# Attention and indexer scores from unsplit q and k, a pair's heads on the two halves of the rows

## The chip, the cores and the metric

The kernel runs on one core of one Trainium2 chip. The metric is the device time of one execution in microseconds. It was taken three times before the change; the median counts.

## What is computed

Two layers (`DEPTH`) of a hybrid block on 256 tokens of width 1024. Each layer projects the normalised input to 6484 columns and feeds four branches: a Mamba-2 branch, and three attention branches of 8 heads with 64 elements each (fox with forget gates, moba, and dsa with an indexer that keeps 64 keys per query). The branches' outputs are gated, projected and summed, and a SwiGLU FFN follows.

```python
DEPTH = 2; SEQ = 256; HEAD_DIM = 64          # 8 heads in fox, moba and dsa, 4 index heads

def fox_branch(q, k, v, f_logit, f_bias):     # causal softmax with a bias cq - cf
    logits = jnp.einsum('bqhd,bkhd->bhqk', qb, k).astype(jnp.float32) * scale
    logits = logits + cq[..., :, None] - cf[..., None, :]
    logits = jnp.where(kpos[None, :] <= qpos[:, None], logits, -jnp.inf)
    p = jax.nn.softmax(logits, axis=-1).astype(v.dtype)
    return jnp.einsum('bhqk,bkhd->bqhd', p, v)

def moba_branch(q, k, v):                     # one block of 256 keys: causal attention
...
def dsa_branch(q, k, v, qi, ki, wi):
    isc = jax.nn.relu(jnp.einsum('bqhd,bkd->bqhk', qib, ki).astype(jnp.float32) * idx_scale)
    isc = jnp.einsum('bqh,bqhk->bqk', wib.astype(jnp.float32) * w_scale, isc)
    isc = jnp.where(kpos[None, None, :] <= qpos[None, :, None], isc, -jnp.inf)
    _, sel = lax.top_k(isc, n_keep)           # n_keep = 64
    ...
    logits = jnp.einsum('bqhd,bqkhd->bqhk', qb, k_sel).astype(jnp.float32) * scale

def hybrid_mixer(...):
    u = h @ w_in                              # 1024 x 6484
    ...                                       # the four branches
    proj = jnp.einsum('bsnc,ncd->bsnd', ys, w_branch)
    gates = jax.nn.sigmoid(h @ w_gate + b_gate).reshape(bsz, seq, N_BRANCH, D_MODEL)
    return jnp.sum(gates * proj, axis=2) @ w_out

def reference(...):
    for l in range(DEPTH):
        h = rms_norm(x, norm_mix_pre[l])
        x = x + rms_norm(hybrid_mixer(h, ...), norm_mix_post[l])
        h = rms_norm(x, norm_ffn_pre[l])
        x = x + rms_norm(swiglu(h, w_ffn_in[l], w_ffn_out[l]), norm_ffn_post[l])
    return x
```

## The kernel before, in words

**Gemms in split form.** Every large product is made of float32r products. A weight is loaded as `raw`, copied by ScalarE to `whi` (line 307), and what the copy lost is subtracted on VectorE to `wlo` (`sub_lo`, line 123). The activations are kept in the same way as a high and a low part (`hh`, `hl`). A gemm adds up high x high, low x high and high x low: `emit_b` makes 24 matmuls of 256 columns for 128 output columns.

**Quanta and ticks.** The work is a list of quanta, each some 24 matmuls of one gemm, in a fixed order. In a mixer it is mv, fv, the small columns, iq (2 quanta), mq (4), mk (4), xs (4), bs (2), cs (2), z (4), fq (4), fk (4), dv, dq, dk, then the gates and branch projections; below, xs2 is the third quantum of xs. The main loop (from line 1134) issues for quantum i the `whi` copy of three quanta ahead and the `wlo` subtraction of two quanta ahead, then the matmuls, then one `tick`. A tick advances every post-processing generator (`posts`) and every active attention generator by one step, so a `yield` means "the next quantum". An engine executes its instructions in the order in which they are issued.

**Attention units.** After the last quantum of mk the four head pairs of moba are put into `units`; the state-space pairs, fox and dsa follow. Every third tick (`STEP`) one unit is started. A unit of `attn_gen` treats two heads, b = 0 and 1, in the steps score (TensorE), low (VectorE: scale, mask and row minimum), expo (ScalarE), recip (VectorE), norm (GpSimd), tr (TensorE), ev (ScalarE), head 1 one tick behind head 0; then come the value product and the split of its result. Ahead of that stand `split_k` and `split_q`, which fill three ticks. They give a product of 128 rows in place of one of 64: the stationary operand `qs` has the query's high part in one half of the rows and its low part in the other, the moving operand `kh` has the key's high part in both, and `klz` has the key's low part in one half and zeros in the other. A head's scores are then two matmuls for each of the two query blocks (128 and 256 keys), and in fox one more each that adds the gate's bias from `csS`.

**The indexer.** `index_gen` makes the scores of four index heads in the same form, sums them with weights into `iacc`, and searches the largest 64 in eight rounds for each query block (`max`, `match_replace` on VectorE), one step a tick. Its result is a mask for dsa.

**The convolution.** The post-processing of xs, bs and cs takes three VectorE steps a quantum (`cacc`, line 585) and one product (`xsc` or `bc`, line 571). That of z has one product, mq and mk have the two steps of `rope`, with GpSimd's part behind them.

**Buffers.** Two pools hold PSUM tiles of one bank each: `pg` has 3 for the gemms, `pa` has 5 for everything else: scores, transposes, value products. Each new tile takes the one that came free first, and its first write waits for the last reader of the old one.

Of the kernel before, what the change touches and what calls it, by code (L numbers as in the profile page):

```python
# [9 lines left out]
F32 = mybir.dt.float32  # L10
# [5 lines left out]
P = 128  # L16
S = 256
# [23 lines left out]
def host_constants():  # L41
    import numpy as np
    c = np.zeros((P, NCST), np.float32)
    p = np.arange(P)
    l = np.arange(S)
    c[:, C_ID:C_ID + P] = np.eye(P, dtype=np.float32)
    c[:, C_TRI:C_TRI + P] = p[:, None] <= p[None, :]
    c[:, C_ONE:C_ONE + P] = 1.0
    c[:, C_MASK:C_MASK + P] = np.where(p[None, :] > p[:, None], BIG, 0.0)
    c[:, C_MASK + P:C_MASK + 3 * P] = np.where(l[None, :] > p[:, None] + P, BIG, 0.0)  # L50
    c[:, C_MASKT:C_MASKT + P] = np.where(p[None, :] < p[:, None], -BIG, 0.0)
    inv = np.power(np.float32(10000.0), -np.arange(0, 64, 2, dtype=np.float32) / np.float32(64)).astype(np.float32)
    ang = (np.arange(S, dtype=np.float32)[:, None] * inv[None, :]).astype(np.float32)
    j = (p % 64) // 2
    c[:, C_COS:C_COS + S] = np.cos(ang).astype(np.float32)[:, j].T
    c[:, C_SIN:C_SIN + S] = np.sin(ang).astype(np.float32)[:, j].T * np.where(p % 2 == 0, -1.0, 1.0)[:, None]
    for r in range(16):
        c[r, C_SEL + r] = 1.0
        c[32 + r, C_SEL + r] = 1.0
    return c  # L60
# [31 lines left out]
def kernel(ctx: ExitStack, tc: tile.TileContext, a, out):  # L92
# [68 lines left out]
    nh = cp.tile([P, 1], F32, name="nh")  # L161
    V.memset(nh, -0.5)
    csS = cp.tile([P, S], F32R, name="csS")
    klz = [cp.tile([P, 2, S], F32R, name=f"klz{i}") for i in range(2)]
    turn = [0]
    par = cp.tile([P, DEPTH, 76], F32, name="par")
    av = cp.tile([P, DEPTH, 16], F32, name="av")
    dsk = cp.tile([P, DEPTH, 4], F32, name="dsk")
# [13 lines left out]

    def clear_pads():
        G.memset(csS.bitcast(F32), 0.0)
        for z in klz:
            G.memset(z.bitcast(F32), 0.0)

    def setup_params():
        V.tensor_copy(sel, cst[:, C_SEL:C_SEL + 16])
        pp = aps()  # L190
        for l in range(DEPTH):
            T.transpose(pp[:, l * P:(l + 1) * P], rows[:, l, :], ident)
        pv = pp[:, 0:2 * P].rearrange("p (l c) -> p l c", l=DEPTH)
        V.tensor_scalar(par[:, :, 0:72], pv[:, :, 0:72], 0.5, None, op0=ALU.mult)
        V.tensor_copy(par[:, :, 72:76], pv[:, :, 72:76])
        V.memset(av, -1.0)
        for l in range(DEPTH):
            ea = tp.tile([P, 8], F32, name="ea")
            A.activation(ea, hd[:, l, 2, :], AF.Exp)
            V.tensor_scalar(av[:, l, 0:8], ea, -1.0, None, op0=ALU.mult)  # L200
            V.tensor_copy(dsk[0:64, l, :], hd[0:64, l, 3, 0:8:2])
            V.tensor_copy(dsk[64:128, l, :], hd[64:128, l, 3, 1:8:2])
# [555 lines left out]

    HALVES = (LOWER, UPPER)

    def split_q(q, scale):
        qs = tp.tile([P, 2, S], F32R, name="qs", bufs=2)
        for b, h in enumerate(HALVES):
            A.activation(qs[h, b, :], q[h], AF.Copy, scale=scale)
        yield
        for b, h in enumerate(HALVES):
            V.scalar_tensor_tensor(qs[HALVES[1 - b], b, :], q[h], scale, qs[h, b, :].bitcast(F32),  # L767
                                   op0=ALU.mult, op1=ALU.subtract)
        return qs

    def split_k(k):
        kh = tp.tile([P, 2, S], F32R, name="kh", bufs=2)
        kl = klz[turn[0] % 2]
        turn[0] += 1
        for b, h in enumerate(HALVES):
            A.activation(kh[h, b, :], k[h], AF.Copy)
        yield
        for b, h in enumerate(HALVES):
            V.tensor_copy(kh[HALVES[1 - b], b, :], kh[h, b, :])
            G.tensor_tensor(kl[h, b, :], k[h], kh[h, b, :].bitcast(F32), op=ALU.subtract)  # L780
        return kh, kl

    def s_mms(ps, b, qs, kh, kl, bias=None):
        for sl, q0, n in QT:
            mm(ps[:, sl], qs[:, b, q0:q0 + P], kh[:, 0:n], True, False)
            mm(ps[:, sl], qs[:, b, q0:q0 + P], kl[:, 0:n], False, bias is None)
            if bias is not None:
                mm(ps[:, sl], selrow(bias), csS[:, 0:n], False, True)

    def index_gen(l, L):  # L790
        yield from wait(("w16", l))
        yield
        ikh = tp.tile([P, S], F32R, name="ikh")
        ikl = tp.tile([P, S], F32R, name="ikl")
        A.activation(ikh, L["ik"], AF.Copy)
        qs = [None, None]
        for i in range(2):
            qs[i] = yield from split_q(L["iq"][:, i, :], 1.0)
        sub_lo(ikl, L["ik"], ikh)
        yield  # L800
        acc = tp.tile([P, 384], F32, name="iacc")
        ps, rl = {}, {}
        for s in range(6):
            if s < 4:
                ps[s] = aps()
                s_mms(ps[s], s % 2, qs[s // 2], ikh, ikl)
            if 0 <= s - 1 < 4:
                rl[s - 1] = t15("irl")
                A.activation(rl[s - 1], ps[s - 1][:, :384], AF.Relu)
            h = s - 2  # L810
            if h >= 0:
                for t, (sl, q0, n) in enumerate(QT):
                    V.scalar_tensor_tensor(acc[:, sl], rl[h][:, sl], L["w16"][:, t, h:h + 1],  # L813
                                           mask[:, sl] if h == 0 else acc[:, sl],
                                           op0=ALU.mult, op1=ALU.subtract if h == 0 else ALU.add)
            yield
        for rnd in range(8):
            for t, (sl, q0, n) in enumerate(QT):
                m8 = tp.tile([P, 8], F32, name="m8", bufs=2)
                V.max(m8, acc[:, sl])  # L820
                V.match_replace(out=acc[:, sl], in_to_replace=m8, in_values=acc[:, sl], imm_value=DROP)  # L821
                yield
        L["dm"] = tp.tile([P, 384], F32, name="dm")
        V.tensor_scalar(L["dm"], acc, DROP * 0.5, BIG, op0=ALU.is_gt, op1=ALU.mult)
        V.tensor_tensor(L["dm"], L["dm"], mask, op=ALU.max)
        flags.add(("dm", l))

    def attn_gen(l, L, br, qk, kk, vk, i, fox, dsa):
        if fox:
            yield from wait(("cs", l))  # L830
        if dsa:
            yield from wait(("dm", l))
        kh, kl = yield from split_k(L[kk][:, i, :])
        qs = yield from split_q(L[qk][:, i, :], -0.125)
        yield
        v = L[vk]
        add = L["dm"] if dsa else mask
        ps, sm, mn, ls, rc, pr, pT, sT = ([None, None] for _ in range(8))

        def score(b):  # L840
            ps[b] = aps()
            s_mms(ps[b], b, qs, kh[:, b, :], kl[:, b, :], 8 + 2 * i + b if fox else None)

        def low(b):
            sm[b] = t15("sm")
            mn[b] = tp.tile([P, 2], F32, name="mn", bufs=4)
            for t, (sl, q0, n) in enumerate(QT):
                V.tensor_tensor_reduce(sm[b][:, sl], ps[b][:, sl], add[:, sl], op0=ALU.add, op1=ALU.min,  # L848
                                       scale=1.0, scalar=3e38, accum_out=mn[b][:, t:t + 1])

        def expo(b):
            pr[b] = tp.tile([P, 384], F32, name="pr", bufs=4)
# [332 lines left out]
```

## Time and profile before

| what | value |
|---|---|
| median of 3 executions | 1130.69 us (1130.31 to 1187.93) |
| the profiled execution | 1132.14 us |
| span of its instructions | 1130.4 us |
| mean granted clock of TensorE | 0.989 |
| busy: TensorE, VectorE, ScalarE, GpSimd | 97%, 68%, 56%, 25% |

The span runs from the first to the last instruction of the profiled execution; the rest of its time lies around it. Busy shares are of the span. Matmuls overlap, and their ends are modelled, so the distance from one start to the next says more than a duration. All times in the rows below are microseconds from the start of the span, unless ns stands there.

### The profile page before, as it was taken

Reading aid. Unit: us, or ns where it says so; the run is one execution under the profiler, and the core shown is the slowest. Engines: PE = TensorE matmul, PEld = TensorE weight load, DVE = VectorE, ACT = ScalarE, POOL = GpSimd, SP = SyncE. Lnnn points to the kernel's source line nnn. Section 1 sums busy time; section 2 is a strip of 40 time slices with the busy share of each in tenths; the row PEclk is TensorE's granted clock in tenths of the full one; section 3 lists DMA queues with packets and bytes.
Section 4 is the critical chain, followed back from the end, with each engine's and each line's share of the span. In section 5 each row is a group of like instructions: output and inputs, shape, how many; then the busy total and the mean of one; then the engine's idle time right before and its main releaser. Section 6 shows DMA issues by size and latency. Waiting matters only on the chain.

```text
span 1130.4 us, 20409 instructions
## 1 busy us (share of the span) xinstructions
PE 1099.5 (97%) x8067; PEld 1031.5 (91%) x8067; DVE 767.1 (68%) x1430; ACT 631.2 (56%) x1190; POOL 277.8 (25%) x327
## 2 busy tenths in 40 slices
PE   7998999999999999999999979999999999999997
PEld 5997889999999799998879979899999988999986
DVE  6799969866547755546478999597754677545542
ACT  6646677676445554445355577757755455454531
POOL 1342337533222100000014424474331320000000
PEclk9998999999999999999999989999999999999999
DMA  7743443454557455556654435345446574565650
GB/s 225 227 150 112 150 149 119 155 163 146 162 191 242 138 185 181 186 188 224 224 141 133 150 112 175 125 135 165 125 155 196 183 238 150 179 195 165 220 194 37
DMA packets 153923, 188.96 MB, mean 167 GB/s; under 512 B 12740, under 2 KB 129764, under 8 KB 153828
## 3 DMA queue, kind: packets, MB, share of 16 engines
q1 hardware_dynamic: 153828, 187.67, 50.7%
q8 instruction: 63, 1.03, 0.4%
q14 instruction: 32, 0.26, 0.1%
HBM read 186.61 MB, written 1.05 MB: 166 GB/s over the span
## 4 chain that ended last, share of the span: by engine, by line
PE 81%; DVE 13%; ACT 3%; issue 2%; POOL 1%; DMA 0%; SPq 0%; DVEq 0%; POOLq 0%; ACTq 0%
PE g L120 61%; PE a L120 18%; DVE wlo L123 4%; DVE cacc L585 2%; PE a L870 2%; ACT junk L238 1%; DVE qs L767 1%; ACT whi L307 1%; DVE rsh L503 1%; POOL pnr L208 1%; DVE iacc L813 0%; DVE rt L504 0%; DVE ny L244 0%; DVE iacc L821 0%; DMA raw<-in_w_in_dram 0%
## 5 line engine op out<-in xcount | busy, mean ns | idle before, releaser
L123 DVE TENSOR_TENSOR wlo<-raw,whi 128x1024 fp32r<-128x1024 f32 (+2 forms) x386 | 444.2, 1170 | 106.6 <-ACT whi L307 84.7
L307 ACT ACTIVATE whi<-raw 128x1024 fp32r<-128x1024 f32 (+2 forms) x386 | 368.6, 986 | 63.9 <-DMA raw<-in_w_ffn_out_dram 37.9
L120 PE MATMUL g<-hh,whi 128*128 128x256 f32 x1776 | 254.9, 287 | 0.0
L120 PE MATMUL g<-hl,whi 128*128 128x256 f32 x1776 | 252.2, 285 | 0.0
L120 PE MATMUL g<-hh,wlo 128*128 128x256 f32 x1776 | 249.6, 283 | 0.0
L120 PEld LDWEIGHTS g<-hh,whi 128*128 128x128 f32 x1776 | 231.0, 193 | 1.3 <-issue 0.7
L120 PEld LDWEIGHTS g<-hl,whi 128*128 128x128 f32 x1776 | 232.1, 194 | 0.0
L120 PEld LDWEIGHTS g<-hh,wlo 128*128 128x128 f32 x1776 | 229.7, 192 | 0.0
L864 POOL TENSOR_SCALAR pr<-pr,rc 128x128 f32<-128x128 f32 x96 | 66.5, 705 | 132.7 <-DVE rc L860 119.0
L150 POOL TENSOR_SCALAR gain<-gain 128x1024 f32<-128x1024 f32 x4 | 4.8, 1207 | 335.6 <-DMA gain<-in_norm_ffn_post_dram 315.0
L643 ACT ACTIVATE gt<-g,par 128x256 f32<-128x256 f32 x64 | 30.3, 474 | 98.8 <-PE g L120 98.8
L663 POOL TENSOR_TENSOR mg<-mg,gt 128x256 f32<-128x256 f32 x48 | 53.5, 1123 | 112.6 <-DVE gt L657 112.6
L1017 DVE TENSOR_TENSOR hu<-gt,g 128x256 f32<-128x256 f32 x40 | 16.9, 421 | 87.0 <-PE g L120 87.0
L120 PE MATMUL a<-whi,hidh 128*128 128x512 f32 x176 | 55.6, 390 | 0.0
L120 PE MATMUL a<-wlo,hidh 128*128 128x512 f32 x176 | 55.5, 389 | 0.0
L120 PE MATMUL a<-whi,hidl 128*128 128x512 f32 x176 | 55.4, 389 | 0.0
L1009 ACT ACTIVATE gt<-g 128x256 f32<-128x256 f32 x40 | 15.4, 385 | 68.0 <-PE g L120 68.0
L506 POOL TENSOR_TENSOR rsh<-rsh,cst 128x256 f32<-128x256 f32 (+1 forms) x38 | 29.5, 777 | 89.3 <-DVE rsh L503 88.9
L657 DVE SCALAR_TENSOR_TENSOR gt<-gt,g 128x256 f32<-128x256 f32 x48 | 19.8, 419 | 40.0 <-PE g L120 34.0
L855 ACT ACTIVATE pr<-sm,mn 128x128 f32<-128x128 f32 x96 | 42.4, 446 | 3.4 <-DVE mn L848 3.4
L120 PE MATMUL g<-whi,hh 128*128 128x512 f32 x128 | 41.3, 404 | 1.6 <-ACT hh L278 1.0
L1019 ACT ACTIVATE hidh<-hu 128x256 fp32r<-128x256 f32 x40 | 16.7, 418 | 45.0 <-DVE hu L1017 45.0
(227 smaller groups left out, 1535.1 us busy)
## 6 DMA issues: line engine op xcount, KB each, us to landing
raw<-in_w_ffn_in_dram SPq DMA_DIRECT2D x40, 1024.0 KB, 5.1
raw<-in_w_in_dram SPq DMA_DIRECT2D x38, 1024.0 KB, 5.0
raw<-in_w_gate_dram SPq DMA_DIRECT2D x32, 1024.0 KB, 5.5
raw<-in_w_ffn_out_dram SPq DMA_DIRECT2D x22, 1024.0 KB, 4.9
raw<-in_w_branch_dram SPq DMA_DIRECT2D x16, 1024.0 KB, 5.0
raw<-in_w_in_dram SPq DMA_DIRECT2D x24, 512.0 KB, 6.3
raw<-in_w_out_dram SPq DMA_DIRECT2D x8, 1024.0 KB, 6.3
raw<-in_w_ffn_in_dram SPq DMA_DIRECT2D x8, 512.0 KB, 5.1
```

Of the source, the lines that this page charges most:

```text
L120: T.matmul(o, l, r, start=start, stop=stop)
L123: V.tensor_tensor(lo, src, hi.bitcast(F32), op=ALU.subtract)
L307: A.activation(dst(c.hi[i]), src(c.raw), AF.Copy)
L506: G.tensor_tensor(sh[:n], sh[:n], sin[:n], op=ALU.mult)
L585: V.scalar_tensor_tensor(ac[:, sft:], u[:, :S - sft], wcol(3 - sft), ac[:, sft:], op0=ALU.mult, op1=ALU.add)
L643: A.activation(th, o, AF.Tanh, bias=par[:, l, 40 + br * 8 + d:41 + br * 8 + d], scale=0.5)
L657: V.scalar_tensor_tensor(L["gt", d], L["gt", d], 1.0, os[j], op0=ALU.add, op1=ALU.mult)
L663: G.tensor_tensor(md, md, L["gt", d], op=ALU.add)
L855: A.activation(pr[b][:, sl], sm[b][:, sl], AF.Exp, bias=mn[b][:, t:t + 1], scale=-1.0, accum_out=ls[b][:, t:t + 1])
L864: G.tensor_scalar(pr[b][:, sl], pr[b][:, sl], rc[b][:, t:t + 1], 1.0, op0=ALU.mult, op1=ALU.mult)
L870: T.transpose(pT[b][:, js], pr[b][:, js], ident)
L1017: V.tensor_tensor(u, H["s", j], o, op=ALU.mult)
```

## The change

The splits of q and k for scores go, with `qs`, `kh`, `klz`, `ikh` and `ikl`. A head's scores become one float32 product of 64 rows for each query block, from the rope results (or, in fox, their copies) directly. Head 0 of a pair has its 64 elements in partitions 0 to 63, head 1 in 64 to 127, so the two lie on the two halves of TensorE's rows. Both heads' scores are issued in one step, each into its own PSUM tile. The factor -1/8 that the split applied to q moves into the instruction of `low`; the masks, the fox bias and the index mask are scaled by -8 to fit. Index heads are treated two at a time in the same way (the index key already stood in both halves of the partitions).

```diff
-    c[:, C_MASK:C_MASK + P] = np.where(p[None, :] > p[:, None], BIG, 0.0)
-    c[:, C_MASK + P:C_MASK + 3 * P] = np.where(l[None, :] > p[:, None] + P, BIG, 0.0)
+    c[:, C_MASK:C_MASK + P] = np.where(p[None, :] > p[:, None], -8 * BIG, 0.0)
+    c[:, C_MASK + P:C_MASK + 3 * P] = np.where(l[None, :] > p[:, None] + P, -8 * BIG, 0.0)
...
-    klz = [cp.tile([P, 2, S], F32R, name=f"klz{i}") for i in range(2)]
-    turn = [0]
...
         G.memset(csS.bitcast(F32), 0.0)
-        for z in klz:
-            G.memset(z.bitcast(F32), 0.0)
...
-        V.memset(av, -1.0)
+        V.memset(av, 8.0)
...
-    def split_q(q, scale):
-        qs = tp.tile([P, 2, S], F32R, name="qs", bufs=2)
...
-    def split_k(k):
-        kh = tp.tile([P, 2, S], F32R, name="kh", bufs=2)
...
-    def s_mms(ps, b, qs, kh, kl, bias=None):
...
+    def scores(q, k, bias=None):
+        ps = [aps(), aps()]
+        for t, (sl, q0, n) in enumerate(QT):
+            for b, h in enumerate(HALVES):
+                mm(ps[b][:, sl], q[h, q0:q0 + P], k[h, 0:n], t == 0, t == 1 and bias is None)
+        if bias is not None:
+            for t, (sl, q0, n) in enumerate(QT):
+                for b in range(2):
+                    mm(ps[b][:, sl], selrow(bias + b), csS[:, 0:n], False, t == 1)
+        return ps
 
     def index_gen(l, L):
         yield from wait(("w16", l))
-        yield
-        ikh = tp.tile([P, S], F32R, name="ikh")
-        ikl = tp.tile([P, S], F32R, name="ikl")
-        A.activation(ikh, L["ik"], AF.Copy)
-        qs = [None, None]
-        for i in range(2):
-            qs[i] = yield from split_q(L["iq"][:, i, :], 1.0)
-        sub_lo(ikl, L["ik"], ikh)
         yield
...
         for s in range(6):
-            if s < 4:
-                ps[s] = aps()
-                s_mms(ps[s], s % 2, qs[s // 2], ikh, ikl)
+            if s in (0, 2):
+                ps[s], ps[s + 1] = scores(L["iq"][:, s // 2, :], L["ik"])
...
-                                           op0=ALU.mult, op1=ALU.subtract if h == 0 else ALU.add)
+                                           op0=ALU.mult, op1=ALU.add)
...
-        V.tensor_scalar(L["dm"], acc, DROP * 0.5, BIG, op0=ALU.is_gt, op1=ALU.mult)
-        V.tensor_tensor(L["dm"], L["dm"], mask, op=ALU.max)
+        V.tensor_scalar(L["dm"], acc, DROP * 0.5, -8 * BIG, op0=ALU.is_gt, op1=ALU.mult)
+        V.tensor_tensor(L["dm"], L["dm"], mask, op=ALU.min)
...
-        kh, kl = yield from split_k(L[kk][:, i, :])
-        qs = yield from split_q(L[qk][:, i, :], -0.125)
-        yield
...
         def score(b):
-            ps[b] = aps()
-            s_mms(ps[b], b, qs, kh[:, b, :], kl[:, b, :], 8 + 2 * i + b if fox else None)
+            if b == 0:
+                ps[:] = scores(L[qk][:, i, :], L[kk][:, i, :], 8 + 2 * i if fox else None)
...
-                                       scale=1.0, scalar=3e38, accum_out=mn[b][:, t:t + 1])
+                                       scale=-0.125, scalar=3e38, accum_out=mn[b][:, t:t + 1])
```

## Rows read from the trace of the kernel before

**Rows 1.** The page: busy time of the engines, and the chain that ended last.

```profile
PE 1099.5 (97%) x8067; PEld 1031.5 (91%) x8067; DVE 767.1 (68%) x1430; ACT 631.2 (56%) x1190; POOL 277.8 (25%) x327
PE 81%; DVE 13%; ACT 3%; issue 2%; POOL 1%; DMA 0%; SPq 0%; DVEq 0%; POOLq 0%; ACTq 0%
```

**Rows 2.** Line 120 (matmuls): TensorE idle until what, us and times.

```profile
  DVE qs L767: 18.9, 10
```

**Rows 3.** Timeline, TensorE, layer 0: start, length, what, count [idle before <-releaser].

```profile
103.48 0.44 PE L120 MATMUL a<-kh,qs 128*128 128x128 f32 x1 [5.22 <-DVE qs L767]
...
117.73 0.33 PE L120 MATMUL a<-kh,qs 128*128 128x128 f32 x1 [1.88 <-DVE qs L767]
```

**Rows 4.** Timeline, TensorE, the second such wait of layer 1.

```profile
673.62 0.33 PE L120 MATMUL a<-kh,qs 128*128 128x128 f32 x1 [1.67 <-DVE qs L767]
```

**Rows 5.** Windows: length, busy us of five engines, TensorE's granted clock, DMA.

```profile
98.30:103.50 5.20, 0.02 (x1) 0.06 (x1) 5.00 (x15) 3.35 (x11) 0.00 (x0) 0.76 0.18 59
103.50:107.90 4.40, 4.40 (x21) 4.40 (x22) 4.26 (x11) 2.85 (x7) 0.24 (x1) 0.51 0.40 118
117.80:122.00 4.20, 4.20 (x23) 4.20 (x24) 4.13 (x9) 4.09 (x12) 0.92 (x1) 0.59 0.22 71
```

**Rows 6.** Timeline, TensorE: one head's scores between two gemms.

```profile
91.88 0.22 PE L120 MATMUL a<-kh,qs 128*128 128x128 f32 x1
91.94 0.27 PE L120 MATMUL a<-klz,qs 128*128 128x128 f32 x1
92.05 0.33 PE L120 MATMUL a<-kh,qs 128*128 128x256 f32 x1
...
92.34 1.12 PE L120 MATMUL g<-hh,whi 128*128 128x256 f32 x8
93.29 1.12 PE L120 MATMUL g<-hl,whi 128*128 128x256 f32 x8
```

**Rows 7.** Timeline, TensorE: full-row float32 products, and the gemm behind them.

```profile
123.12 1.47 PE L120 MATMUL a<-bc 128*128 128x256 f32 x8
124.35 1.20 PE L120 MATMUL g<-hh,whi 128*128 128x256 f32 x8
```

**Rows 8.** Timeline, TensorE: a pair's value product, and the gemm behind it.

```profile
182.27 0.88 PE L120 MATMUL a<-sT,xdt 128*64 128x256 f32 x8
183.08 1.21 PE L120 MATMUL g<-hh,whi 128*128 128x256 f32 x8
```

**Rows 9.** Timeline, GpSimd: the two subtractions for pair 0.

```profile
88.96 2.62 POOL L780 TENSOR_TENSOR klz<-mk,kh 64x256 fp32r<-64x256 f32 x2 [8.46 <-ACT kh L776]
```

**Rows 10.** Timeline, VectorE, in the convolution quanta of layer 0.

```profile
80.71 1.21 DVE L123 TENSOR_TENSOR wlo<-raw,whi 128x1024 fp32r<-128x1024 f32 x1
...
83.27 0.74 DVE L813 SCALAR_TENSOR_TENSOR iacc<-irl,w,iacc 128x128 f32<-128x128 f32 x2
84.04 0.61 DVE L779 CAST kh<-kh 64x256 fp32r<-64x256 f32 x2
...
90.01 0.96 DVE L571 SCALAR_TENSOR_TENSOR xsc<-th,cacc 128x256 f32<-128x256 f32 x1
90.90 2.00 DVE L585 SCALAR_TENSOR_TENSOR cacc<-cu,par,cacc 128x255 f32<-128x255 f32 x3
...
94.80 0.42 DVE L571 SCALAR_TENSOR_TENSOR xsc<-th,cacc 128x256 f32<-128x256 f32 x1
95.14 1.51 DVE L585 SCALAR_TENSOR_TENSOR cacc<-cu,par,cacc 128x255 f32<-128x255 f32 x3
...
101.39 0.42 DVE L820 MAX8 m<-iacc 128x8 f32<-128x256 f32 x1
...
102.25 0.28 DVE L848 CUSTOM_DVE_ANT_0 sm<-a,cst 128x128 f32<-128x128 f32 x1
...
102.91 0.87 DVE L767 SCALAR_TENSOR_TENSOR qs<-mq,qs 64x256 fp32r<-64x256 f32 x2
...
118.16 1.23 DVE L123 TENSOR_TENSOR wlo<-raw,whi 128x1024 fp32r<-128x1024 f32 x1
```

More of the change, by code (lines that the diff above doesn't have):

```diff
@@ L759 @@
     HALVES = (LOWER, UPPER)
-    def split_q(q, scale):
-        qs = tp.tile([P, 2, S], F32R, name="qs", bufs=2)
-        for b, h in enumerate(HALVES):
-            A.activation(qs[h, b, :], q[h], AF.Copy, scale=scale)
-        yield
[L766 to L769, printed above, removed]
-    def split_k(k):
-        kh = tp.tile([P, 2, S], F32R, name="kh", bufs=2)
[L773 to L776, printed above, removed]
-        yield
[L778 to L781, printed above, removed]
-    def s_mms(ps, b, qs, kh, kl, bias=None):
[L784 to L788, printed above, removed]
+    def scores(q, k, bias=None):
[8 more added lines that the diff above has]
+        return ps
     def index_gen(l, L):
         yield from wait(("w16", l))
-        yield
-        ikh = tp.tile([P, S], F32R, name="ikh")
-        ikl = tp.tile([P, S], F32R, name="ikl")
-        A.activation(ikh, L["ik"], AF.Copy)
-        qs = [None, None]
-        for i in range(2):
-            qs[i] = yield from split_q(L["iq"][:, i, :], 1.0)
-        sub_lo(ikl, L["ik"], ikh)
         yield
@@ L832, in attn_gen @@
             yield from wait(("dm", l))
-        kh, kl = yield from split_k(L[kk][:, i, :])
-        qs = yield from split_q(L[qk][:, i, :], -0.125)
-        yield
         v = L[vk]
```

## The prediction, on record before the result

> **What bounds the kernel now.** I read the page first: matmuls keep TensorE busy 97% of the span, and they are most of the chain that ended last, with VectorE next at 13% [rows 1]. So a change counts by what it takes from TensorE's stream and by the waits in it. The second view lists what ended TensorE's idle times: 18.9 us, matmuls and weight loads together, ended with `qs`, the split query that line 767 writes on VectorE [rows 2]. TensorE's timeline shows where. In layer 0 the first product of moba pair 1 waits 5.22 us and that of pair 2 1.88 us [rows 3]; layer 1 repeats both, the second with 1.67 us [rows 4]. From start to start each costs some 0.15 us more than its idle time.
>
> The windows show what comes with such a wait. During the first, VectorE is busy 5.00 of 5.20 us: TensorE waits because VectorE is behind with everything. Afterwards the granted clock is 0.51 of full (the 1.2 GHz level), and 21 matmuls take 4.40 us; after the second wait 23 take 4.20 us at 0.59 [rows 5]. At the usual pace, eight gemm products in 0.95 us [rows 6], these are 2.4 and 2.7 us, so the clock costs 2.0 and 1.5 us. Layer 0 thus loses 5.4 + 2.0 + 2.0 + 1.5 = 10.9 us here, layer 1 some 10.7: 21.6 us, the only large sum that the change can reach.
>
> **TensorE's own work.** A head's scores now take four matmuls, from 91.88 to 92.34 us [rows 6], so 0.92 us a pair (fox adds its bias, which stays). The new pair is four float32 products of 64 rows. The trace has no product of 64 rows, but two neighbours with the same columns (two of 256, two of 128); each float32 product shows as two matmuls. The four full-row products of `bc` in `ssd_prep_gen` are eight matmuls and take 1.23 us [rows 7]. The value products of a pair go to two halves of the columns: again eight, in 0.81 us [rows 8]. So the halves overlap, though all products of one half are written first. Leaving costs something: the gemm group behind lasts 1.21 us where its kind lasts 1.12 [rows 6, 8], and I take the same 0.09 us for entering. A visit costs 0.99 us. The load ahead of the first product has 128 columns, where the value product's has 64; full-row matmuls of 128 columns start 0.11 us apart (91.94 to 92.05), so half of that shows more. I take 1.05 us, +0.13 a pair, since halves of the rows are nearest to halves of the columns. The ends: half of 1.23, 0.62 us (overlap, and neither entry nor exit: -0.30), and 1.23 + 0.18 + two loads of 0.11 = 1.63 us (no overlap: +0.71). Between them: loads of the two halves one behind the other, 8 x 0.11 + 0.18 + the last product, 0.2, = 1.26 us (+0.34).
>
> The Trainium skill (TensorE: Matmul & The Clock Gate, "LDWEIGHTS") says that a load's time goes by its columns and not by its rows, about 107 ns for 128; by that eight loads one behind the other are an estimated 0.86 us. The Trainium skill (TensorEngine Tiling, "Key Properties") says that tiles load and multiply in parallel, which speaks for 1.05 us. The trace has overlapping loads of 64 columns and none of 64 rows, so it decides for neither.
>
> **What leaves the other engines.** For an attention pair ScalarE loses four copies, GpSimd two subtractions (2.62 us for two, beside VectorE [rows 9]) and VectorE two casts, together 0.61 us, and two splits, 0.87 us [rows 10]. `low` keeps its cost: -0.125 stands where 1.0 stood in the same instruction. Masks, `av` and the two cleared pads are set-up that no wait of the list in [rows 2] hangs on.
>
> **What moves.** The split's suspensions go, so a pair's scores come three quanta earlier, and the indexer's too. Their inputs are no wait: pair 0's rope results are written three quanta before. But VectorE's `low`, the search's rounds and GpSimd's `norm` move with them, into the convolution quanta where VectorE is late. And both heads take their PSUM tiles at once.
>
> **The sum in the convolution quanta.** Between the wlo subtractions of quanta xs2 (80.71) and z2 (118.16) VectorE spends 37.45 us on eight quanta [rows 10].
> - Removed: three pairs' casts, 3 x 0.61 = 1.8; three splits, 3 x 0.87 = 2.6; the indexer's last product step, 0.74, now done earlier; and the stretching beside GpSimd's subtractions, where a product took 0.96 us instead of 0.42 and three `cacc` steps 2.00 instead of 1.51 [rows 9, 10]: 1.0, and once more 0.5. Together 6.6.
> - Added: two more `low` steps, 2 x 0.66 (102.25 to 102.91); one more search round, 0.86 (101.39 to 102.25); two reciprocals, some 0.1; two more `norm` steps on GpSimd, whose stretching I put at 1.0 (bounds 0 and 2, by the stretching just named). Together 3.3.
>
> That leaves 37.45 - 6.6 + 3.3 = 34.1 us. For the same quanta TensorE needs 8 x 2.87 us for gemms of 24, two pairs at 1.05, three times three transposes at 0.11 and a value product at 0.99: 27.1 us. VectorE starts xs2 up to 1 us behind. So at z2 it is about 34.1 + 0.5 - 27.1 = 7.5 us behind; TensorE comes to the scores of pair 3 after a gemm and three transposes, 3.2 us later.
>
> **The wait that takes its place.** The five PSUM tiles of pool `pa` go round in the order in which they come free. At z2, pair 0's value product and pair 1's two transposes hold three. Pair 3's scores need both of pair 2's score tiles, and the second is read by `low(1)`, issued in quantum z1 as VectorE's last work there. So pair 3 waits until VectorE ends z1, just as `qs` made pair 2 wait: 7.5 - 3.2 = 4.3 us. Behind the waiting product stand the gemm of z3 and all later matmuls, in order. Pairs 1 and 2 find tiles freed two quanta back or more, and their waits go. After z2 no convolution step is left and VectorE catches up. With 1.6 us for the clock, by the two measured, a layer still loses 5.9 us: two layers gain 21.6 - 11.8 = 9.8 us. An error of 0.3 us in each quantum moves a layer by 2.4 us.
>
> The extra 0.13 us counts only where TensorE doesn't wait for VectorE anyway: not for the index pairs and moba pairs 0 to 2, so for 18 of 28 pairs, +2.3 us. Sum: -7.5 us. The profiled execution took 1132.14 us, of which the span is 1130.4; the median is 1130.69, and I set the difference against that: 1123.2, say 1123 us. Two per cent, 22.6 us, is about what a measurement of this kernel can tell from no change.
>
> **Rivals.**
> 1. The waits vanish. If VectorE's backlog at z2 stays within 3.2 us (no stretching, each quantum 0.4 us cheaper), 21.6 us come back, less 28 x 0.13 = 3.6: 1112.7 us; with pairs at 0.62 us, 1100.7. For: VectorE loses 24 x 1.48 + 4 x 0.87 = 39 us over the kernel. Against: the sum above. Chance 0.18.
> 2. The row halves don't overlap. From 0.92 + 9.8/18 = 1.46 us a pair on the change loses; at 1.63 it is 18 x 0.71 - 9.8 = +3.0: 1133.7 us, slower than before. For: the trace has no such product. Against: column halves overlap, and the two heads write different PSUM tiles. Chance 0.17.
> 3. Loads one behind the other: 18 x 0.34 - 9.8 = -3.7: 1127 us. Chance 0.10.
> 4. The change doesn't do what it says: the wait for a PSUM tile takes back all that the wait for `qs` cost. It needs VectorE 12 us behind at z2, not 7.5. Then +2.3 is left: 1133 us. Chance 0.12.
>
> My forecast, 1117 to 1129, has 0.43. The range takes in rival 1 without its far end and rivals 2 to 4: 1109 to 1137. Faster by over 2% (below 1108) needs rival 1 and cheap pairs at once: 0.09. Slower by over 2% needs over 1 us more for each of 28 pairs than I forecast: 0.03. Within 2%: 0.88.
>
> **What would show it.** No wait for `qs`; none of 5 us ahead of pair 1; one of 3 to 6 us ahead of pair 3's second head, ended by `sm` or `mn` of VectorE's line 848, with a granted clock near 0.5 behind it; eight score matmuls of 64 rows in some 0.85 us, the halves starting almost together; VectorE with about 39 us less work. I am wrong if that wait is under 1.5 us or over 8, if a pair takes over 1.3 us between its two gemms, or if TensorE waits for GpSimd's `pr` ahead of the transposes.

## The result, and the profile after

The changed kernel takes 1116.16 us, the median of four executions (1115.65 to 1118.65), where the kernel before takes 1130.5 us, the median of four beside them. The difference of the medians is 14.3 us. The ratio is 0.988 with a 95% interval of 0.986 to 0.990, so 11 to 15 us less. (The ratio leaves out one disturbed execution of the kernel before, which the medians hold; without it their difference is 14.2 us.) The forecast was 7.5 us less. The profiled execution of the changed kernel took 1115.65 us, its span is 1113.6 us, and the mean granted clock is 0.999 where it was 0.989.

The page of the changed kernel, busy time of the engines and the chain that ended last; its lines answer to [rows 1]:

```profile
PE 1094.3 (98%) x8067; PEld 1013.4 (91%) x8067; DVE 712.2 (64%) x1324; ACT 588.4 (53%) x1084; POOL 239.0 (21%) x277
PE 81%; DVE 12%; ACT 2%; issue 2%; DMA 2%; POOL 1%; SPq 1%; DVEq 0%; POOLq 0%; ACTq 0%
```

TensorE has as many instructions as before and is still the bound. VectorE has 54.9 us less work, ScalarE 42.8 and GpSimd 38.8. VectorE's removed instructions took 48.7 us in the kernel before (18.8 for `kh`, 29.0 for `qs`, 0.9 for `ikl`), more than the 39 us that the prediction made of one pair's prices, since many of them were longer than those of that pair. The other 6.2 us went from instructions that stayed, among them the convolution steps beside GpSimd's subtractions; I did not take them apart further.

What ended TensorE's idle times at line 120 in the changed kernel (us, times; matmuls and weight loads together), the answer to [rows 2]:

```profile
  issue: 9.5, 41
  DVE mn L814: 5.9, 4
```

No `qs` is left, since there is no such tile, and its 18.9 us have become 5.9 us for `mn`, which `low` writes (line 814 now, 848 before). For matmuls alone it was 14.0 us and is 2.7. TensorE's timeline of the changed kernel shows where that is: first one undisturbed visit to the scores, then the places in layer 0 and layer 1 that answer to [rows 3, 4]:

```profile
86.32 1.12 PE L120 MATMUL g<-hh,wlo 128*128 128x256 f32 x8
87.37 0.93 PE L120 MATMUL a<-mk,mq 64*128 64x128 f32 x8
88.23 1.22 PE L120 MATMUL g<-hh,whi 128*128 128x256 f32 x8
89.28 0.88 PE L120 MATMUL g<-hl,whi 128*128 128x256 f32 x6
...
108.99 0.48 PE L120 MATMUL a<-mk,mq 64*128 64x128 f32 x2
111.43 0.92 PE L120 MATMUL a<-mk,mq 64*128 64x128 f32 x6 [1.96 <-DVE mn L814]
112.28 0.98 PE L120 MATMUL g<-hh,whi 128*128 128x256 f32 x6
...
658.40 0.49 PE L120 MATMUL a<-mk,mq 64*128 64x128 f32 x2
659.68 0.92 PE L120 MATMUL a<-mk,mq 64*128 64x128 f32 x6 [0.79 <-DVE mn L814]
660.53 0.74 PE L120 MATMUL g<-hh,whi 128*128 128x256 f32 x4
```

At 87.37 us the eight score matmuls run to the next gemm in 0.86 us. At 108.99 us pair 3 gets out two matmuls, the first product of head 0; the next product is head 1's and needs the second PSUM tile, and it starts only at 111.43. From 108.99 to the next gemm at 112.28 the visit takes 3.29 us, 2.43 more than 0.86; in layer 1 (658.40 to 660.53) it is 1.27 more. The two together cost 3.7 us. (Where an expectation below puts them at 2.1 and 1.0 us, it counts only to the start of head 1's products, and leaves out that six matmuls then take as long as eight, since head 0's can no longer overlap with them.) VectorE's timeline of the changed kernel shows what the product waited for:

```profile
110.74 0.28 DVE L814 CUSTOM_DVE_ANT_0 sm<-a,cst 128x128 f32<-128x128 f32 x1
110.95 0.08 DVE L814 DVE_READ_ACCUMULATOR2_ANT mn<- 128x1 f32 x1
110.95 0.42 DVE L814 CUSTOM_DVE_ANT_0 sm<-a,cst 128x256 f32<-128x256 f32 x1
111.29 0.08 DVE L814 DVE_READ_ACCUMULATOR2_ANT mn<- 128x1 f32 x1
111.29 1.22 DVE L123 TENSOR_TENSOR wlo<-raw,whi 128x1024 fp32r<-128x1024 f32 x1
```

That is `low(1)` of pair 2. It ends at 111.37 us, and the product starts at 111.43.

The windows during and behind that wait in the changed kernel (length, busy us of five engines, granted clock, DMA share, GB/s), the answer to [rows 5]:

```profile
109.40:111.40 2.00, 0.08 (x1) 0.00 (x0) 1.93 (x10) 1.37 (x5) 0.00 (x0) 1.00 1.04 349
111.40:115.90 4.50, 4.47 (x34) 4.08 (x35) 4.47 (x11) 4.47 (x12) 1.88 (x2) 1.00 0.20 67
```

VectorE is still busy all through the wait, 1.93 of 2.00 us, so it is still what is late. But the granted clock stays at 1.00 (2.4 GHz) behind it in this execution, where it stood at 0.51 and 0.59 before.

Where the time came from, by layer: the list of line 120 gives the first and the last start of the FFN's second product, which lie in layer 0 and at the end of layer 1 (duration min/median/max in ns, then first to last start in us). Before the change:

```profile
L120 PE MATMUL a<-whi,hidh x176: 389/389/476, 508.4 to 1123.3; 128*128 128x512 f32 x176
```

After it:

```profile
L120 PE MATMUL a<-whi,hidh x176: 389/389/476, 499.1 to 1106.6; 128*128 128x512 f32 x176
```

Up to layer 0's FFN 9.3 us are gained, from there to the end 614.9 - 607.5 = 7.4 us. Of the 9.3 us, 1.0 lies ahead of everything that was changed: the mixer's first gemm starts at 36.18 us in this execution, at 37.19 in that of before. So the two layers give 8.3 and 7.4 us, 15.7 together in the profiled executions, 14.3 between the medians.

### The profile page after: what moved, and what is told of

It is laid out like the page before. It is cut to its first block, busy times and chain, and to the rows that moved or that the text cites. A ratio compares the mean times of both kernels' runs of the same rounds, so it can differ in the third digit from the quotient of the medians.

```text
span 1113.6 us, 20105 instructions
## 1 busy us (share of the span) xinstructions
PE 1094.3 (98%) x8067; PEld 1013.4 (91%) x8067; DVE 712.2 (64%) x1324; ACT 588.4 (53%) x1084; POOL 239.0 (21%) x277
## 3 DMA queue, kind: packets, MB, share of 16 engines
HBM read 186.61 MB, written 1.05 MB: 169 GB/s over the span
## 4 chain that ended last, share of the span: by engine, by line
PE 81%; DVE 12%; ACT 2%; issue 2%; DMA 2%; POOL 1%; SPq 1%; DVEq 0%; POOLq 0%; ACTq 0%
PE g L120 61%; PE a L120 18%; DVE wlo L123 4%; DVE cacc L581 2%; DMA raw<-in_w_in_dram 2%; PE a L836 1%; ACT whi L303 1%; ACT junk L234 1%; DVE iacc L790 1%; DVE iacc L782 1%; DVE sm L814 1%; POOL pnr L204 1%; DVE rsh L499 1%; DVE m L789 1%; DVE ny L240 0%
## 5 line engine op out<-in xcount | busy, mean ns | idle before, releaser
L120 PE MATMUL g<-hl,whi 128*128 128x256 f32 x1776 | 249.3, 283 | 0.0
L120 PEld LDWEIGHTS g<-hh,whi 128*128 128x128 f32 x1776 | 227.9, 191 | 8.0 <-DVE rc L826 1.3
L120 PEld LDWEIGHTS g<-hl,whi 128*128 128x128 f32 x1776 | 229.0, 192 | 0.0
L830 POOL TENSOR_SCALAR pr<-pr,rc 128x128 f32<-128x128 f32 x96 | 71.3, 754 | 153.8 <-DVE rc L826 131.8
```

The lines of the kernel that those rows point to most:

```text
L120: T.matmul(o, l, r, start=start, stop=stop)
L830: G.tensor_scalar(pr[b][:, sl], pr[b][:, sl], rc[b][:, t:t + 1], 1.0, op0=ALU.mult, op1=ALU.mult)
```

## The experiments

My theory was that of the prediction: what is gained is VectorE's time in the convolution quanta, and with it TensorE's waits; TensorE itself works longer for a pair. The rivals were that the scores themselves had become cheaper on TensorE, that the gain is that scores no longer depend on a split, that the earlier start of the pairs brings it, and that the wait at pair 3 is general lateness and not the PSUM tile. Beside the experiments the kernel before took 1131.7 to 1131.8 us; ratios are to that. Where two changed kernels are compared, it is by their medians; the kernel before took 1.2 us more beside the experiments than beside the result, and by so much such a difference can be off. Unless said otherwise, an edit is to the changed kernel.

**VectorE's load back.** Two casts and two subtractions a pair, as the splits had them, into tiles that nothing reads.

```diff
+        def extra(s):
+            if s == 1:
+                kx = tp.tile([P, 2, S], F32R, name="kx", bufs=2)
+                for b, h in enumerate(HALVES):
+                    V.tensor_copy(kx[HALVES[1 - b], b, :], L[kk][h, i, :])
+            if s == 2:
+                qx = tp.tile([P, 2, S], F32R, name="qx", bufs=2)
+                for b, h in enumerate(HALVES):
+                    V.scalar_tensor_tensor(qx[HALVES[1 - b], b, :], L[qk][h, i, :], -0.125, L[qk][h, i, :],
+                                           op0=ALU.mult, op1=ALU.subtract)
...
+            extra(s)
             yield
```

> The changed kernel with the two casts and two splits of every attention pair put back on VectorE, into tiles that nothing reads. Load theory (the gain is VectorE's lost work in the convolution quanta): three pairs' 1.48 us, 4.4 us in all, lengthen the wait at pair 3 of each layer from 2.1 and 1.0 us to 5 to 6 us, with the clock down behind it: 1116 + 2 x 4.4 + 2 x 1.6 = 1126 to 1130 us. Dependence theory (the gain is that no score waits for a split any more, whatever VectorE does): no change, 1116 us. TensorE theory (the 64-row products are what is cheaper): 1116 us too.

Measured: 1128.84 us, 0.997 (0.995 to 0.998). 12.7 of the 14.3 us are gone, though TensorE's instructions are those of the changed kernel. The wait at pair 3 in layer 0 has grown, by the timeline of TensorE in this kernel:

```profile
115.86 1.64 PE L120 MATMUL a<-mk,mq 64*128 64x128 f32 x6 [3.20 <-DVE mn L814]
```

and the window behind it shows the clock at the lower level:

```profile
116.00:120.00 4.00, 4.00 (x18) 3.35 (x19) 3.92 (x10) 3.97 (x10) 0.55 (x1) 0.50 0.30 103
```

VectorE's load is thus enough to make nearly the old time out of the new one, though no score depends on a split here. These 3.20 us of idle have the half clock behind them, as the waits before the change had. Part of the 12.7 us is that clock: the eight executions fall into three of 1125.5 to 1125.9 us at a mean granted clock of 0.996, and five of 1128.3 to 1130.4 at 0.991 to 0.993.

**GpSimd's load back.** Two subtractions a pair on GpSimd, into a tile that nothing reads.

```diff
+        def extra(s):
+            if s == 1:
+                kx = tp.tile([P, 2, S], F32R, name="kx", bufs=2)
+                for b, h in enumerate(HALVES):
+                    G.tensor_tensor(kx[h, b, :], L[kk][h, i, :], L[qk][h, i, :], op=ALU.subtract)
...
+            extra(s)
             yield
```

> The changed kernel with two GpSimd subtractions of 64x256 for every attention pair put back, one quantum after its scores, into a tile that nothing reads. If they stretch VectorE as beside the first pair before (1.0 us a pair): the wait at pair 3 grows by some 3 us a layer, with the clock perhaps: 1122 us (1120 to 1126). If GpSimd's work costs VectorE next to nothing: 1116 us.

Measured: 1122.94 us, 0.992 (0.989 to 0.994), 6.8 us more than the changed kernel. VectorE gets no instruction more, but those beside the subtraction last longer. The timelines of VectorE and of GpSimd in this kernel:

```profile
92.15 2.01 DVE L581 SCALAR_TENSOR_TENSOR cacc<-cu,par,cacc 128x255 f32<-128x255 f32 x3
...
92.98 1.78 POOL L846 TENSOR_TENSOR kx<-mk,mq 64x256 fp32r<-64x256 f32 x2
```

Three `cacc` steps take 2.01 us, 1.51 alone [rows 10] and 1.64 at this place in the changed kernel, where `norm` runs beside them; the waits for `mn` grow from 5.9 to 7.8 us, and the granted clock in the window that holds the one of layer 0 is 0.72:

```profile
110.00:116.00 6.00, 4.10 (x18) 3.09 (x19) 5.86 (x18) 4.71 (x15) 0.33 (x1) 0.72 0.57 175
```

VectorE's load is worth 12.7 us and GpSimd's 6.8, 19.5 together, where gain and price of the pairs make 14.3 + 3.6 = 17.9. They need not add up exactly, as the clock comes and goes with them: the one execution here at a mean granted clock of 0.999 took 1118.11 us, the three at 0.992 to 0.994 took 1122.7 to 1123.8. The copies that ScalarE lost were not put back by themselves; what they were worth is not shown, but the two loads together leave little for them to explain.

**The earlier start undone.** Three suspensions ahead of each pair and of the indexer, as many as the splits had.

```diff
         if dsa:
             yield from wait(("dm", l))
+        yield
+        yield
+        yield
```

> The changed kernel with the three quanta between a unit's start and its scores put back as empty steps, for the indexer too. Load theory: VectorE has 3.3 us less to do before quantum z2 and falls back less, so the waits of 2.1 and 1.0 us at pair 3 go: 1113 us (1112 to 1115). Early-start theory (the gain comes from scores that come three quanta earlier): most of the gain is lost, 1125 us or more.

Measured: 1113.11 us, 0.984 (0.982 to 0.985): 3.05 us faster than the changed kernel, whose two waits at pair 3 cost 3.7. Among the costliest of TensorE's idle times `mn` no longer stands. The earlier start is no gain; it is a loss of some 3 us.

**`low` of both heads in one quantum.** Then the second score tile is free a quantum earlier.

```diff
         def low(b):
+            if b == 0:
+                low_of(0)
+                low_of(1)
+
+        def low_of(b):
             sm[b] = t15("sm")
```

> The changed kernel with the low step of both heads in the quantum after their scores, so that the second score tile is free a quantum earlier. PSUM theory (pair 3 waits for the tile that low of pair 2's second head still reads): both waits go, 1116 - 3.1 = 1113 us, with none of line 814 left over 0.5 us. If TensorE waits there for something else that VectorE is late with: 1116 us, and the wait stays with another name.

Measured: 1113.14 us, 0.984 (0.983 to 0.986). The timeline of TensorE in this kernel, at pair 3 and behind it:

```profile
109.08 0.93 PE L120 MATMUL a<-mk,mq 64*128 64x128 f32 x8
109.94 1.21 PE L120 MATMUL g<-hh,whi 128*128 128x256 f32 x8
...
115.03 0.89 PE L120 MATMUL a<-bc 128*128 128x256 f32 x4 [1.30 <-DVE bc L567]
```

All eight matmuls go out at once: the wait was for that tile. VectorE is still late, which shows a quantum later, where the state-space products wait 1.30 us for the convolution's result. That was not foreseen; it costs less than what went. Both remedies in one kernel:

> The changed kernel with both remedies of the wait at pair 3: low of both heads together, and scores three quanta later. Each alone gave 1113 us. If that wait is all that was left: 1113 us again, nothing added. If something else of VectorE's backlog remains: 1111 us or less.

Measured: 1113.64 us, 0.984 (0.982 to 0.986): nothing is added, since both remove the same wait.

**Both heads on one half of the rows.** The second head takes the first head's q and k.

```diff
-            for b, h in enumerate(HALVES):
+            for b, h in enumerate((LOWER, LOWER)):
                 mm(ps[b][:, sl], q[h, q0:q0 + P], k[h, 0:n], t == 0, t == 1 and bias is None)
```

> The changed kernel with both heads' scores made from the lower half of the rows: the second head takes the first head's q and k, so its output is another. Same columns, same count, no second half. Overlap theory: the visit of a pair to TensorE grows from 0.86 us to that of full rows or a little more, 1.25 to 1.5 us, so 28 x 0.4 to 0.65 = 11 to 18 us: 1127 to 1134 us. If a half alone runs as fast (the order of issue or the loads set the pace): 1116 us.

Measured: 1129.85 us, 0.998 (0.997 to 0.999). The timeline of TensorE in this kernel, one visit:

```profile
89.27 1.57 PE L120 MATMUL a<-mk,mq 64*128 64x128 f32 x8
90.77 0.98 PE L120 MATMUL g<-hh,whi 128*128 128x256 f32 x6
```

1.50 us to the next gemm, where two halves take 0.86. With the same matmuls the halves save 0.64 us a pair, 28 x 0.64 = 17.9 us; of that 13.7 show, because a slower TensorE covers most of what VectorE is late (waits for `mn` 1.5 us, not 5.9). So without the overlap nearly the whole gain would be spent.

**Every score product twice.**

```diff
-        for t, (sl, q0, n) in enumerate(QT):
-            for b, h in enumerate(HALVES):
-                mm(ps[b][:, sl], q[h, q0:q0 + P], k[h, 0:n], t == 0, t == 1 and bias is None)
+        for rnd in range(2):
+            for t, (sl, q0, n) in enumerate(QT):
+                for b, h in enumerate(HALVES):
+                    mm(ps[b][:, sl], q[h, q0:q0 + P], k[h, 0:n], t == 0, t == 1 and (rnd == 0 or bias is None))
```

> The changed kernel with every score product made twice into the same tile (the second clears the first; the fox bias once). It prices four float32 products of 64 rows without the entry and the exit. By the column halves a pair grows by 0.64 us: 28 x 0.64 = 17.9 us less the 3.1 us of waits at pair 3 that it covers: 1131 us. If TensorE had slack in the attention steps: well under 1125 us.

Measured: 1130.24 us, 0.999 (0.998 to 1.000). The timeline of TensorE in this kernel:

```profile
89.08 1.58 PE L120 MATMUL a<-mk,mq 64*128 64x128 f32 x16
90.59 0.62 PE L120 MATMUL g<-hh,whi 128*128 128x256 f32 x3
```

Eight matmuls more take 0.65 us more, 18.2 us for 28 pairs; 14.1 show, again because the longer visits cover what VectorE is late: no wait for `mn` is left. The scores are a price that TensorE pays at once, not a saving.

**All products of head 0 first.**

```diff
-        for t, (sl, q0, n) in enumerate(QT):
-            for b, h in enumerate(HALVES):
+        for b, h in enumerate(HALVES):
+            for t, (sl, q0, n) in enumerate(QT):
```

> The changed kernel with all products of head 0 written ahead of those of head 1, as the value products are. If TensorE itself takes the halves side by side, in whatever order they are written: a visit stays at 0.86 us, 1116 us. If the change needs the alternating order: visits of up to 1.5 us, 1130 us.

Measured: 1117.6 us, 0.987 (0.985 to 0.989). The timeline of TensorE in this kernel:

```profile
88.67 0.93 PE L120 MATMUL a<-mk,mq 64*128 64x128 f32 x8
89.53 0.74 PE L120 MATMUL g<-hh,whi 128*128 128x256 f32 x4
```

0.86 us again: the halves overlap in either order. At pair 3 this execution shows something else, by the timeline of TensorE and the window behind the wait:

```profile
112.63 0.92 PE L120 MATMUL a<-mk,mq 64*128 64x128 f32 x4 [1.41 <-DVE mn L814]
113.47 1.45 PE L120 MATMUL g<-hh,whi 128*128 128x256 f32 x8
...
117.94 1.47 PE L120 MATMUL a<-bc 128*128 128x256 f32 x8
```

```profile
114.20:117.70 3.50, 3.50 (x19) 3.50 (x18) 3.43 (x11) 2.61 (x5) 2.07 (x2) 0.51 0.11 13
```

The same wait has the half clock behind it here. From 113.47 to 117.94 us 24 gemm matmuls take 4.47 us, where the usual distances make 1.05 + 2 x 0.96 = 2.97: the clock costs 1.5 us, close to the 1.6 that the prediction added for it.

**The search left out, before and after.** The search is VectorE work of about one step a quantum in the same stretch.

```diff
         for rnd in range(8):
             for t, (sl, q0, n) in enumerate(QT):
-                m8 = tp.tile([P, 8], F32, name="m8", bufs=2)
-                V.max(m8, acc[:, sl])
-                V.match_replace(out=acc[:, sl], in_to_replace=m8, in_values=acc[:, sl], imm_value=DROP)
                 yield
```

> The kernel before, with the indexer's 16 search steps left out (their 16 quanta stay as empty steps), so dsa keeps every key. Seven of the steps, about 0.72 us each, lie in VectorE's convolution quanta: 5 us a layer. Load theory: the waits for the split query, with the clock behind them 10.9 us a layer, shrink by 5 us at least and by most of it if the clock stays up: 1131 - 10 to -20 = 1111 to 1121 us, though no score, split or wait is changed. Dependence theory (scores wait for the split because it comes one quantum ahead of them): 1131 us.

> The changed kernel with the same 16 search steps left out. Load theory: only the 3.1 us of waits at pair 3 are left to be had: 1113 us, so that the change, without the search, gains little or loses: the pairs' 28 x 0.13 = 3.6 us show. Dependence or TensorE theory: the change still gains its 14 us over the kernel before without the search.

Measured: 1121.9 us before the change, 0.992 (0.990 to 0.993), and 1113.93 us after it, 0.984 (0.983 to 0.985). The first is just above what I expected: waits for `qs` have shrunk from 18.9 to 8.0 us and not gone. The timeline of TensorE in the kernel before without the search:

```profile
100.97 0.45 PE L120 MATMUL a<-kh,qs 128*128 128x128 f32 x1 [2.67 <-DVE qs L767]
```

So the search's work alone doesn't make VectorE late; with it gone the splits still do. With less on VectorE the change brings 8.0 us, with more 14.3. That it would then bring little, which I had expected, is wrong by what is left of the waits. After the change, no wait for `mn` remains without the search.

**The splits of the kernel before, moved off VectorE.** Casts to ScalarE, subtractions to GpSimd (with the factor and the masks of the changed kernel, so that the subtraction has no factor).

```diff
-                V.tensor_copy(kh[HALVES[1 - b], b, :], kh[h, b, :])
+                A.activation(kh[HALVES[1 - b], b, :], k[h], AF.Copy)
...
-            V.scalar_tensor_tensor(qs[HALVES[1 - b], b, :], q[h], scale, qs[h, b, :].bitcast(F32), ...)
+            G.tensor_tensor(qs[HALVES[1 - b], b, :], q[h], qs[h, b, :].bitcast(F32), op=ALU.subtract)
```

> The kernel before with the split products kept, but nothing of the attention splits on VectorE: the second copy of the key on ScalarE, the query's low part on GpSimd (the factor and the masks as in the changed kernel; the index key's one subtraction stays). Scores, suspensions and the dependence on a split are those of before. Load theory: VectorE is relieved of 4.4 us a layer in the convolution quanta, and the waits for the split, 10.9 us a layer with the clock, shrink by 5 to 8 us unless four subtractions on GpSimd stretch VectorE by as much: 1115 to 1122 us. Dependence theory: 1131 us or slower, for GpSimd's subtraction takes longer than VectorE's.

Measured: 1125.82 us, 0.995 (0.994 to 0.997): a gain, but smaller than I expected. The timeline of TensorE in this kernel:

```profile
106.64 0.33 PE L869 MATMUL a<-cst,pr 128*128 128x128 f32 x1 [2.10 <-POOL pr L863]
...
119.03 1.19 PE L120 MATMUL a<-bc 128*128 128x256 f32 x4 [1.86 <-ACT sT L873]
```

Waits for `qs` have come down from 18.9 to 2.1 us, but the transposes now wait for GpSimd's `norm`, and the state-space products for ScalarE. The load has to go, not to move: here it makes two other engines late. The scores still depend on a split in this kernel, and the waits for it are all but gone: that dependence alone did not make them.

## Why the prediction was right, and where it was off

The time lies in the stated range, 1109 to 1137 us, but just below the band called my forecast, 1117 to 1129, and the gain is nearly twice the forecast. Of the signs named, the end of the waits for `qs`, the place of the new wait and the length of a pair's matmuls came as said. The new wait did not: 2.4 and 1.3 us where 3 to 6 stood, in layer 1 under the 1.5 us named as a sign of being wrong; the half clock behind it did not come in the profiled execution; and VectorE lost 54.9 us of work, not 39. The prediction also took 2% for about the least that can be told from no change; the interval of the ratio is 0.2% either way.

1. *What bounds the kernel.* Right. The waits for `qs` and the half clock behind them, 21.6 us, were the sum that the change could reach, and VectorE's lateness was their cause: its load put back takes 12.7 of the 14.3 us away.

2. *The price of a pair on TensorE.* Right. In the rows from 86.32 us on, the gemm group ahead of the visit takes 1.05 us to the next start, where its kind takes 0.96; the visit takes 0.86 us, and the group behind it 1.05 again (88.23 to 89.28). So 0.09 + 0.86 + 0.09 = 1.04 us, where 1.05 was forecast (+0.13 a pair), as taken from the value product's two column halves. The other kinds of pair agree, from start to start: a dsa pair takes 0.86 us where its two heads took 0.55 and 0.46, with 0.17 more to enter behind transposes and 0.10 to leave; a fox pair with its bias products takes 1.42 where 0.77 and 0.69 stood, with 0.17 to enter and nothing to leave. That is +0.12 and +0.13. The rule that tiles load and multiply in parallel (the Trainium skill, TensorEngine Tiling, "Key Properties") agrees with the two visits of 0.86 and 1.50 us. Rivals 2 and 3 fall with this.

3. *VectorE in the convolution quanta.* The mechanism was right, several terms were mis-sized. From the wlo of xs2 to that of z2 VectorE takes 32.60 us, not 34.1, and 32.61 in layer 1; TensorE takes 27.07 us from gemm to gemm in both layers, 27.1 forecast. The rows of the two engines at both ends, layer 0 (its last wlo, at 111.29, is shown above) and layer 1:

```profile
78.55 1.22 PE L120 MATMUL g<-hh,whi 128*128 128x256 f32 x8
78.69 1.21 DVE L123 TENSOR_TENSOR wlo<-raw,whi 128x1024 fp32r<-128x1024 f32 x1
...
105.62 1.20 PE L120 MATMUL g<-hh,whi 128*128 128x256 f32 x8
...
626.93 1.22 DVE L123 TENSOR_TENSOR wlo<-raw,whi 128x1024 fp32r<-128x1024 f32 x1
627.95 1.22 PE L120 MATMUL g<-hh,whi 128*128 128x256 f32 x8
...
655.02 1.20 PE L120 MATMUL g<-hh,whi 128*128 128x256 f32 x8
659.54 1.22 DVE L123 TENSOR_TENSOR wlo<-raw,whi 128x1024 fp32r<-128x1024 f32 x1
```

Four terms of VectorE's sum make the 1.5 us. The `low` steps were read as 0.66 us with a split behind them [rows 10]; with a wlo behind them they take 0.55 from start to start (110.74 to 111.29), so that four at 0.66 became six at 0.55: +0.6 us, not +1.3. The stretching for `norm` on GpSimd was put at 1.0 us, from the stretching beside subtractions. VectorE in the changed kernel, beside `norm` at 90.13 and 94.07 us and alone at 108.46:

```profile
91.40 1.64 DVE L581 SCALAR_TENSOR_TENSOR cacc<-cu,par,cacc 128x255 f32<-128x255 f32 x3
...
95.60 0.61 DVE L567 SCALAR_TENSOR_TENSOR xsc<-th,cacc 128x256 f32<-128x256 f32 x1
...
108.46 1.51 DVE L581 SCALAR_TENSOR_TENSOR cacc<-cu,par,cacc 128x255 f32<-128x255 f32 x3
```

That is 0.13 and 0.19 us for a pair's two `norm` steps. From 78.69 to 111.29 lie two pairs' `norm` steps, 0.64 us in all, and no other stretching is left there: 0.4 us less than the sum had. Casts and splits cost more from start to start than they last; two wlo rows of the kernel before, behind the cast at 84.04 and the split at 102.91 [rows 10], show 0.65 and 0.90 us:

```profile
84.69 1.23 DVE L123 TENSOR_TENSOR wlo<-raw,whi 128x1024 fp32r<-128x1024 f32 x1
...
103.81 1.23 DVE L123 TENSOR_TENSOR wlo<-raw,whi 128x1024 fp32r<-128x1024 f32 x1
```

All six took 4.7 us and not 4.4. The search round more cost 0.7 us and not 0.86. Besides, VectorE did not start 0.5 us behind: it started 0.14 us behind in layer 0 and 1.02 ahead in layer 1. So at z2 it is 5.7 us behind in layer 0 and 4.5 in layer 1, not 7.5.

4. *The wait that takes its place.* Right in place, cause and queue: pair 3's second head, a PSUM tile that `low(1)` of pair 2 reads as VectorE's last work of quantum z1. Issuing that earlier removes it, and so does the later start. Its size was off by the backlogs of step 3 alone: with the measured ones the same working gives 5.7 - 3.2 = 2.5 us and 4.5 - 3.2 = 1.3, and 2.4 and 1.3 were measured; the forecast was 4.3 each.

5. *The clock.* I added 1.6 us a layer, and in the profiled execution nothing of it came: the windows show a granted clock of 1.00 behind the wait, and its mean is 0.999. That is no property of the change. With the products in the other order the profiled execution has the same wait with 0.51 behind it and pays 1.5 us. The four executions of the changed kernel had mean granted clocks of 0.999, 0.998, 0.998 and 0.995, and the last of these is the longest, 1118.65 us; where its clock fell is not known. So the term was right in size where it came, and that it stayed away here was not foreseen.

6. *For how many pairs the price counts.* Off by 1.3 us: I counted 18 of 28, since the others lie ahead of a wait. But both waits, the measured ones and the forecast one, are already net of TensorE's own time, and so the 0.13 us counts for all 28, 3.6 us.

With these the sum gives -21.6 + 3.7 + 3.6 = -14.3 us, the difference of the medians. That it fits to the tenth is luck: the interval is 11 to 15 us, and the layers of the two profiled executions, from which its terms are read, differ by 15.7. Of the 6.8 us that the forecast missed, the smaller wait makes 4.9 (8.6 forecast for both layers, 3.7 measured) and the clock 3.2, less the 1.3 of step 6. The result lies between the forecast, 1123.2 us, and rival 1 (all waits vanish, 1112.7 us), and nearer to the rival: the kernels without the wait at pair 3 took 1113.1.

The fastest version found is the changed kernel with either remedy, 1113.1 us, 0.984 of before.

## What to carry to other kernels

When an engine beside the bound is late in one stage, a change is to be costed there, quantum by quantum: here work was bought off VectorE for 3.6 us of TensorE, and 17.9 us of waits, with the clock behind them, went. Look next at what the freed time makes late: a step that starts earlier brings its own work into the crowded stage, and a PSUM tile that is handed on holds TensorE until its slowest reader is through. Adding the removed work back into scratch tiles, engine by engine, tells in one run each whose time the gain was.

## What the runs showed of the hardware

- The clock behind an idle of 1.4 to 2 us goes either way. Before the change 1.88 us of idle were followed by 0.59; after it, 1.96 us left the clock at 1.00; in the changed kernel with the products of head 0 first, 1.41 us were followed by 0.51. In the kernel with the splits moved, 2.10 us for `pr` left it at 1.00 and 1.86 us for `sT` were followed by 0.57. The length of the idle alone doesn't decide it, and what does was not tried.
- What a GpSimd instruction costs a VectorE step depends on when it ends. Three `cacc` steps take 1.51 us alone, 1.64 beside `norm` and, in the kernel with GpSimd's load back, 2.01 beside `norm` and a subtraction. The last of those three steps, the subtraction beside it, and the same step alone in the changed kernel:

```profile
93.31 0.85 DVE L581 SCALAR_TENSOR_TENSOR cacc<-cu,par,cacc 128x253 f32<-128x253 f32 x1
92.98 0.90 POOL L846 TENSOR_TENSOR kx<-mk,mq 64x256 fp32r<-64x256 f32 x1
...
109.48 0.48 DVE L581 SCALAR_TENSOR_TENSOR cacc<-cu,par,cacc 128x253 f32<-128x253 f32 x1
```

  The step starts while the subtraction runs and ends 0.28 us after it (94.16 and 93.88). So do all ten `cacc` steps that start beside a subtraction for `kx` in this kernel or for `klz` in the kernel before the change; beside `norm` it is 0.26 to 0.27 us. The `low` steps, which read the scores from PSUM, are at most 0.03 us longer there. The Trainium skill (SBUF — State Buffer, "SBUF: two separate sides") calls the port that VectorE and GpSimd share an exclusive lock, also for a VectorE operation with two inputs in SBUF while GpSimd reads SBUF, and says that the engine that comes second is fully blocked. The trace agrees for these steps, whose two tensors lie in SBUF: what looks like stretching is a wait for the end of GpSimd's instruction.
- Float32 products on the two halves of the rows overlap almost wholly, in this shape: eight matmuls on one half take 1.50 us, on two halves 0.86, entry and exit 0.1 us each beside gemms; sixteen on two halves take 1.51 us. The two orders tried give the same 0.86.
